# The front of a streaming-encoder kernel on one core: w_ada and x loads alternated, one shift sum moved to VectorE, two powers joined

## Chip, core and metric

The kernel runs on one core of a Trainium2 chip. The metric is the device time of one execution in microseconds. Before the change three runs took 1591.05, 1592.59 and 1591.18 us, with a median of 1591.18. The engines carry these names in the profile: PE is TensorE (matrix products; PEld is its loading of weights), DVE is VectorE, ACT is ScalarE, POOL is GpSimd, SP is SyncE, which here only issues DMAs.

## The reference

One inference step of a two-branch streaming encoder layer, over 1024 prompt rows and 32 sample rows, with D = 1024. What the change touches is the start: the modulation by the condition vector c, and the first normalised input h of the input projection.

```python
def rmsnorm(x, g):
    xf = x.astype(jnp.float32)
    y = xf * lax.rsqrt(jnp.mean(xf * xf, axis=-1, keepdims=True) + EPS)
    return (y * g.astype(jnp.float32)).astype(x.dtype)

def trunk_layer(x, c, ...):
    mod = jax.nn.silu(c) @ w_ada + b_ada
    sh1, sc1, gt1, sh2, sc2, gt2 = jnp.split(mod[:, None, :], 6, axis=-1)

    h = rmsnorm(x, g_mix) * (1 + sc1) + sh1
    u = h @ w_in
    ...
```

Behind this stand a chunk-band attention, an mLSTM memory, their merge, an output projection and a SwiGLU block, each of which the change leaves as it is. There are two condition vectors: one for the 1024 prompt rows, one for the 32 sample rows.

## The kernel before

x is held transposed: eight "features" of 128 channels lie on the partitions (KD = 8), and the 1056 rows of both sequences lie along the free axis, cut into three tiles of 352 (TILES). The first two tiles together, 704 columns, are the early part (CUT = 704); the last 352 columns are the late part, whose last 32 belong to the sample sequence.

The front (`first_units`) does this:

- **Loads.** SP issues them in the order in which they are written. `load_ada` (L248) loads one feature of w_ada as two DMAs of 512 KB: part 0 holds the scale's weights, part 1 the shift's. `xTs[j][:, :CUT]` (L265) is the early part of feature j of x, 352 KB. `load_first` (L255) loads half of each of the first three weight blocks of w_in, and L270 the late columns of x.
- **Shift and scale.** `ada_sums(j, part, pt)` (L321) sums one part of one feature on TensorE: eight matrix products of 128x128, each in two records of the profile, with silu(c) broadcast as the moving operand (L324). `ada_done(j)` (L328) lets ScalarE evict scale (`s1`, L329) and shift (`sh1`, L330).
- **Row norms.** `square_sum` squares a feature on ScalarE (L300) and adds it on VectorE (L302). `token_sums` sums over the partitions on TensorE (L307), `token_roots` (L310) divides on VectorE (L315 to L318) and takes the power -0.5 on GpSimd (L319). The early 704 rows form two groups of three columns, the late ones a third. `spread` transposes the roots (L230) and ScalarE copies them to RB (L233).
- **Weights.** Products of f32 operands are made in three passes from a high and a low part. `first_high` (L426) writes the high part on ScalarE, `first_low` (L430) the low part on VectorE.
- **h.** `scaled_x` (L338 on VectorE; L340 on GpSimd for the sample's 32 columns) multiplies x by scale and root, `high_h` (L348; L350 and L351 for the sample) adds the shift on ScalarE and writes the high part, `low_h` (L357; L359) the low part.
- **Products.** `products(k, q)` (L480) makes pass q of feature k for the first three weight blocks and both early tiles. The features run k = 0 to 7. In the code of the loop stand, between the passes, the scaled rows of feature k + 2, the low parts of k + 1, the squares of the late columns, and from k = 3 on the late roots and the late part of h. Then come the late products and `put_k`, `put_v`, `put_q`, which evict on ScalarE and VectorE (L605, L608, L610, L646, L692, L708, L710); then units of further blocks (L405), transposes of v (L680), the head splits (L668, L671), and attention (L800 and behind).

The order on TensorE, ScalarE, VectorE and GpSimd is the order in which the code is written. Each engine works through its own list in order and waits at an instruction until what it needs is there. Tiles of the pool `slots` (16 of them, named `s` in the profile) and PSUM tiles of the pool `mm` (three) are used again when their last reader is done.

## Time and profile before

| | us |
|---|---|
| median of three runs | 1591.18 |
| the profiled execution, its own time | 1591.2 |
| its span, first to last instruction | 1589.5 |
| first matrix product | 5.14 |
| token sums of the early rows (L307) | 29.69 |
| first product with h (L480) | 35.73 |
| sums of feature 7 (L324 into psS), begin | 37.15 |
| late products begin (psS, L480) | 64.60 |

The profile is of one execution. A row of the timeline gives the start of a group of like instructions, its length, the engine, the source line, the operation, the tile written and the tiles read, and in brackets how long the engine stood idle before it and what ended that. The span is the time from the first to the last instruction; the execution's own time is 1.7 us longer, for what lies around it. The same difference is used for the forecast.

### The profile page before, as it was taken

Reading aid. Unit: us, or ns where it says so; the run is one execution under the profiler, and the core shown is the slowest. Engines: PE = TensorE matmul, PEld = TensorE weight load, DVE = VectorE, ACT = ScalarE, POOL = GpSimd, SP = SyncE. Lnnn points to the kernel's source line nnn. Section 1 sums busy time; section 2 is a strip of 40 time slices with the busy share of each in tenths; the row PEclk is TensorE's granted clock in tenths of the full one; section 3 lists DMA queues with packets and bytes.
Section 4 is the critical chain, followed back from the end, with each engine's and each line's share of the span. In section 5 each row is a group of like instructions: output and inputs, shape, how many; then the busy total and the mean of one; then the engine's idle time right before and its main releaser. Section 6 shows DMA issues by size and latency. Waiting matters only on the chain.

```text
span 1589.5 us, 27294 instructions
## 1 busy us (share of the span) xinstructions
PE 1566.5 (99%) x10197; PEld 1549.4 (97%) x10197; DVE 1104.4 (69%) x2276; ACT 788.3 (50%) x1743; POOL 422.1 (27%) x439
## 2 busy tenths in 40 slices
PE   8999999999999999999999999999999999999997
PEld 8999999999999999999999999999999999999997
DVE  3765565556766835446655699898898986799755
ACT  4765554544555545444434656544445444545443
POOL 0433343342223311000012100665565750000000
PEclk9999999999999999999999999999999999999999
DMA  9322233343132323685353312223222227427444
GB/s 373 98 78 83 88 98 101 96 131 107 41 91 74 91 74 100 122 271 172 114 156 112 94 55 67 82 69 105 69 86 89 68 86 250 137 80 250 131 136 156
DMA packets 176337, 186.03 MB, mean 117 GB/s; under 512 B 11750, under 2 KB 141450, under 8 KB 176206
## 3 DMA queue, kind: packets, MB, share of 16 engines
q1 hardware_dynamic: 173542, 182.45, 36.6%
q10 hardware_dynamic: 2664, 1.85, 0.4%
q8 instruction: 80, 1.31, 0.4%
q14 instruction: 51, 0.42, 0.1%
HBM read 150.11 MB, written 34.17 MB: 116 GB/s over the span
## 4 chain that ended last, share of the span: by engine, by line
PE 91%; DVE 3%; ACT 2%; issue 2%; DMA 2%; POOL 1%; ACTq 0%; SPq 0%; DVEq 0%; POOLq 0%
PE mm L405 41%; PE psb L1875 18%; PE mm L1875 11%; PE psb L2257 3%; PE mm L954 3%; PE mm L2257 2%; PE psV L859 2%; PE psb L2121 2%; PE psS L800 2%; PE psT L827 1%; PE mm L2121 1%; DMA s<-in_w_ada_dram 1%; DMA s<-in_x_dram 1%; PE psV L1188 1%; PE psT L1190 1%
## 5 line engine op out<-in xcount | busy, mean ns | idle before, releaser
L405 PE MATMUL mm<-s,wsp 128*128 128x352 f32 x4104 | 687.2, 324 | 0.1
L405 PEld LDWEIGHTS mm<-s,wsp 128*128 128x128 f32 x4104 | 657.3, 188 | 1.9 <-issue 0.4
L368 DVE TENSOR_TENSOR wsp<-wraw,wsp 128x512 fp32r<-128x512 f32 (+1 forms) x280 | 236.4, 861 | 117.3 <-ACT wsp L367 114.1
L1875 PE MATMUL psb<-s,wsp 128*128 128x352 f32 x1611 | 271.7, 322 | 1.5 <-DVE wsp L368 0.8
L367 ACT ACTIVATE wsp<-wraw 128x512 fp32r<-128x512 f32 x336 | 199.5, 617 | 139.9 <-PE psb L1875 43.0
L1875 PEld LDWEIGHTS psb<-s,wsp 128*128 128x128 f32 x1611 | 260.6, 188 | 2.1 <-DVE wsp L368 1.1
L1875 PE MATMUL mm<-s,wsp 128*128 128x352 f32 x933 | 159.3, 322 | 0.0
L1875 PEld LDWEIGHTS mm<-s,wsp 128*128 128x128 f32 x933 | 151.2, 188 | 0.5 <-DVE wsp L368 0.5
L820 POOL TENSOR_SCALAR st<-st,mx 128x640 f32<-128x640 f32 (+5 forms) x72 | 53.5, 743 | 183.4 <-DVE mx L819 165.4
L1281 DVE CUSTOM_DVE_ANT_0 junk<-wa,t 128x512 bf16<-128x512 f32 x128 | 94.8, 741 | 5.6 <-DMA wa<-in_w_mod_dram 4.6
L368 POOL TENSOR_TENSOR wsp<-wraw,wsp 128x512 fp32r<-128x512 f32 x56 | 74.5, 1351 | 52.5 <-ACT wsp L367 50.2
L814 DVE CUSTOM_DVE_ANT_0 st<-psS,bias 128x640 f32<-128x640 f32 (+5 forms) x72 | 44.5, 618 | 57.4 <-PE psS L800 43.5
L815 ACT ACTIVATE st<-st,mx 128x640 f32<-128x640 f32 (+5 forms) x72 | 47.9, 666 | 64.4 <-DVE mx L814 64.2
L1822 POOL TENSOR_TENSOR t<-t,sl 128x352 f32<-128x352 f32 x19 | 18.4, 967 | 212.8 <-ACT sl L1820 212.8
L834 ACT ACTIVATE pT<-psT 128x640 fp32r<-128x640 f32 (+3 forms) x80 | 38.6, 493 | 64.2 <-PE psT L827 51.7
L2230 POOL TENSOR_TENSOR fst<-fst,mhalf 128x6 f32<-128x6 f32 x1 | 2.3, 2315 | 221.1 <-DVE fst L2229 221.1
L839 DVE TENSOR_TENSOR pT<-psT,pT 128x640 fp32r<-128x640 f32 (+3 forms) x80 | 44.0, 558 | 21.4 <-ACT pT L834 21.3
L1494 POOL TENSOR_TENSOR wraw<-wraw,raw 128x512 f32<-128x512 f32 x33 | 55.8, 1705 | 0.9
L954 PE MATMUL mm<-s,s 128*128 128x264 f32 (+3 forms) x432 | 54.5, 283 | 0.0
L2257 PE MATMUL psb<-s,wsp 128*128 128x352 f32 x330 | 54.2, 324 | 0.0
L2257 PEld LDWEIGHTS psb<-s,wsp 128*128 128x128 f32 x330 | 53.1, 188 | 0.1
L954 PEld LDWEIGHTS mm<-s,s 128*128 128x128 f32 (+1 forms) x432 | 51.9, 179 | 0.5
(374 smaller groups left out, 2462.0 us busy)
## 6 DMA issues: line engine op xcount, KB each, us to landing
wraw<-in_w_in_dram SPq DMA_DIRECT2D x37, 512.0 KB, 3.6
wraw<-in_w_gate_up_dram SPq DMA_DIRECT2D x33, 512.0 KB, 3.9
wa<-in_w_mod_dram SPq DMA_DIRECT2D x64, 256.0 KB, 2.7
wraw<-in_w_down_dram SPq DMA_DIRECT2D x32, 512.0 KB, 4.5
a_d<-t SPq DMA_DIRECT2D x22, 528.0 KB, 2.7
g_d<-t SPq DMA_DIRECT2D x16, 528.0 KB, 5.1
t<-g_d SPq DMA_DIRECT2D x16, 528.0 KB, 4.6
s<-in_w_ada_dram SPq DMA_DIRECT2D x16, 512.0 KB, 7.7
```

The lines of the kernel that those rows point to most:

```text
L367: act.activation(dst[:, 0], src, AF.Copy)
L368: eng.tensor_tensor(dst[:, 1], src, f(dst[:, 0]), op=ALU.subtract)
L405: pe.matmul(pt[:, :hi - lo], wt[(w0 + k) // 4][:, a, (w0 + k) % 4], xt[k][:, b, lo:hi], start=(k == 0 and q == 0), stop=(k == n - 1 and q ...
L814: dve.tensor_tensor_reduce(so, sv, bi, -1.0, 3.0e38, ALU.add, ALU.min, mx[:n, 1:2])
L815: act.activation(st[:n, :w], st[:n, :w], AF.Exp, bias=mx[:n, 1:2], scale=-1.0, accum_out=mx[:n, 2:3])
L820: pool.tensor_scalar(st[:n, :w], st[:n, :w], mx[:n, 3:4], 1.0, op0=ALU.mult, op1=ALU.mult)
L954: pe.matmul(pt[:n, :wd], hs[k][:, a, i * P:i * P + n], whl[b][:, k, :wd], start=(k == 0 and q == 0), stop=(k == KD - 1 and q == 2))
L1281: dve.tensor_tensor_reduce(junk, wa, crow[:, c], 1.0, 0.0, ALU.mult, ALU.add, at)
L1494: self.eng.tensor_tensor(a(dst), a(x), a(y), op=op)
L1875: pe.matmul(acc, wt[:, a, k], x[k][:, b], start=(start and not onto and k == 0 and q == 0), stop=(stop and k == 3 and q == 2), skip_group_ ...
L2121: pe.matmul(acc, wt[k // 4][:, u, k % 4], piece_of[k, i][:, v], start=(k == 0 and q == 0), stop=(k == KP - 1 and q == 2))
L2257: pe.matmul(acc, wt[(k - k0) // 4][:, u, (k - k0) % 4], piece_of[k, 2][:, v], start=(k == 0 and q == 0), stop=(k == NF - 1 and q == 2))
```

## The change

Four things are edited.

1. The loads of w_ada and x alternate. `load_ada(n)` now issues one half of a feature; the table `x_behind` says behind which half a row of x is issued. Part 1 of feature 7 comes last, behind the second halves of the first weights, and ahead of it a new DMA brings silu(c) of both sequences, broadcast to all partitions (`silb`, 1 MB). The squares are spread over the features by the table `squares`.
2. The shift of feature 7 is no longer summed by TensorE. Its weights are laid out anew by the host (output channel on the partition), and `shift_sum` multiplies them by `silb` and sums along the free axis on VectorE, one pass for each sequence, at k = 3 and k = 4 of the products. `ada_done(7)` evicts the scale alone.
3. `powers` takes the power of both early groups in one operation of six columns. The late group keeps its own.
4. The three `first_high` and `first_low` of the first halves now stand ahead of `spread`, and the scaled rows and high parts of feature 0 behind the second sums of feature 6.

```diff
--- before.py
+++ after.py
@@ -245,27 +245,28 @@
     def in_block(c):
         return w_in[(c - GA) // P + 28 if c >= GA else c // P]
 
-    def load_ada():
-        j = len(was)
-        wa = slot([P, 2, D])
-        for i in range(2):
-            sp.dma_start(wa[:, i], w_ada[i, j])
-        was.append(wa)
+    def load_ada(n):
+        j, i = divmod(n, 2)
+        if i == 0:
+            was.append(slot([P, 2, D]))
+        sp.dma_start(was[j][:, i], w_ada[i, j])
+
+    def load_x(j):
+        sp.dma_start(xTs[j][:, :CUT], x_t[j][:, :CUT])
 
     def load_first(half):
         for raw, c in zip(first_ws, first_cols):
             sp.dma_start(raw[:, 4 * half:4 * half + 4], in_block(c)[:, 4 * half:4 * half + 4])
 
     sq2 = slot([P, 2, T])
-    for _ in range(5):
-        load_ada()
-    for j in range(KD):
-        if j == 5:
-            load_ada()
-        sp.dma_start(xTs[j][:, :CUT], x_t[j][:, :CUT])
-    load_ada()
+    x_behind = {1: 0, 2: 1, 4: 2, 5: 3, 7: 4, 8: 5, 9: 6, 10: 7}
+    for n in range(13):
+        load_ada(n)
+        if n in x_behind:
+            load_x(x_behind[n])
     load_first(0)
-    load_ada()
+    load_ada(13)
+    load_ada(14)
     for i, xp in enumerate(xTp):
         sp.dma_start(xp[:, :, CUT:], x_t[2 * i:2 * i + 2].rearrange("n p t -> p n t")[:, :, CUT:])
     load_first(1)
@@ -276,6 +277,7 @@
     silu1 = cp.tile([P, 2], F32, name="silu1")
     sh1 = cp.tile([P, 2, KD], F32, name="sh1")
     s1 = cp.tile([P, 2, KD], F32, name="s1")
+    shs = cp.tile([P, 2], F32, name="shs")
     gm1 = cols[:, R_GMIX:R_GMIX + KD]
     psA, psH, psS = ps_t(), ps_v(), ps_s()
     tok = psS[:, 512:]
@@ -316,7 +318,10 @@
         else:
             dve.tensor_scalar(x[:, 0, :2], p3[:, :2], 1.0 / D, EPS, op0=ALU.mult, op1=ALU.add)
             dve.tensor_scalar(x[:m, 0, 2:], p3[:m, 2:], 1.0 / D, EPS, op0=ALU.mult, op1=ALU.add)
-        pool.tensor_tensor(x[:, 1], x[:, 0], mhalf[:, :3], op=ALU.pow)
+
+    def powers(t0, t1):
+        x = roots[:, :, 3 * t0:3 * t1]
+        pool.tensor_tensor(x[:, 1], x[:, 0], mhalf[:, :3 * (t1 - t0)], op=ALU.pow)
 
     def ada_sums(j, part, pt):
 
@@ -325,8 +330,16 @@
                       was[j][:, part, k * P:(k + 1) * P], csil[:, k].unsqueeze(1).to_broadcast([P, DH, 2]),
                       start=(k == 0), stop=(k == KD - 1), skip_group_check=True)
 
+    def shift_sum(j, c, silb):
+
+        at = shs[:, c:c + 1]
+        dve.tensor_tensor_reduce(was[j][:, 0], was[j][:, 1], silb[:, c], 1.0, 0.0, ALU.mult, ALU.add, at)
+        dve.tensor_tensor(sh1[:, c, j:j + 1], at, cols[:, R_ADA + j:R_ADA + j + 1], op=ALU.add)
+
     def ada_done(j, pt):
         act.activation(s1[:, :, j], pt[:, :2], AF.Identity, scale=gm1[:, j:j + 1], bias=gb1[:, j:j + 1])
+        if j == KD - 1:
+            return
         act.activation(sh1[:, :, j], pt[:, P:P + 2], AF.Identity, bias=cols[:, R_ADA + j:R_ADA + j + 1])
 
     hs = []
@@ -436,21 +449,22 @@
         silu_cols()
         act.activation(crows, crows, AF.Silu)
         act.dma_start(sil_d, crows)
+        silb = slot([P, 2, D])
+        sp.dma_start(silb, bass.AP(sil_d.tensor, sil_d.offset, [[0, P], [D, 2], [1, D]]))
+        load_ada(15)
+        squares = ((0,), (1,), (2, 3), (4,), (5, 6), (7,))
         for j in range(6):
             pt = mmt()
             ada_sums(j, 0, pt)
             ada_sums(j, 1, pt)
-            if j < 3:
-                ada_done(j, pt)
-            else:
-                n = {3: 2, 4: 6, 5: KD}[j]
-                for i in range({3: 0, 4: 2, 5: 6}[j], n):
-                    square_sum(i, 0, CUT)
-                ada_done(j, pt)
+            for i in squares[j]:
+                square_sum(i, 0, CUT)
+            ada_done(j, pt)
         token_sums(0, CUT, 0, DH)
         groups = [(0, 3 * P), (3 * P, CUT)]
         for i, (lo, hi) in enumerate(groups):
             token_roots(i, hi - lo, 3 * DH * i, DH)
+        powers(0, 2)
         pt = mmt()
 
         def spread(i):
@@ -458,19 +472,17 @@
             bcast_cols(RB, roots[:, 1, 3 * i:3 * i + 3], [min(P, hi - a) for a in range(lo, hi, P)], lo)
 
         ada_sums(6, 0, pt)
-        first_high(0, 0)
-        first_high(1, 0)
+        for i in range(3):
+            first_high(i, 0)
+        for i in range(3):
+            first_low(i, 0)
         spread(0)
         spread(1)
-        scaled_x(0, *early[0])
-        scaled_x(0, *early[1])
-        first_high(2, 0)
-        high_h(0, *early[0])
-        high_h(0, *early[1])
         ada_sums(6, 1, pt)
+        for t in range(2):
+            scaled_x(0, *early[t])
+            high_h(0, *early[t])
         ada_done(6, pt)
-        for i in range(3):
-            first_low(i, 0)
         pts = [[mmt(), mmt()], [psA[:, :512], psA[:, 512:]], [mmt(), psH]]
         last = [psS[:, :512], tok]
 
@@ -498,7 +510,6 @@
             for i in range(3):
                 product(0, i, 0, t)
         ada_sums(7, 0, psS)
-        ada_sums(7, 1, psS)
         scaled_x(1, 0, CUT)
         low_h(0, 0, CUT)
         high_h(1, 0, CUT)
@@ -539,10 +550,13 @@
             if k == 3:
                 token_sums(late[0], NT, NT, 32)
                 token_roots(2, NT, NT, 32)
+                powers(2, 3)
                 W.loaded = W.split_n = 3
                 W.load(6)
                 early_loads.append(cache_loads())
                 early_loads.extend(rel_bias_tile(h) for h in range(2))
+            if k in (3, 4):
+                shift_sum(7, k - 3, silb)
             if k == 4:
                 for i, n in enumerate((P, P, NT - 2 * P)):
                     pe.transpose(tok[:, i * P:i * P + n], roots[:n, 1, 6 + i:7 + i].to_broadcast([n, P]), ident[:n, :n])
@@ -2309,7 +2323,9 @@
             a = a.T.reshape(KD, P, T)
         elif name == "w_ada":
             a = _np.asarray(inputs["w_ada"])[0, :, :2 * D].reshape(KD, P, 2, KD, P)
-            a = a.transpose(2, 3, 1, 0, 4)[::-1].reshape(2, KD, P, D)
+            last = a[:, :, 0, -1].reshape(D, P).T
+            a = a.transpose(2, 3, 1, 0, 4)[::-1].reshape(2, KD, P, D).copy()
+            a[1, -1] = last
         else:
             a = _np.asarray(inputs[name])
         if name == "rel_bias":
```

The list of SP at the start, before. The tiles s_106, s_109, s_112, s_115, s_118, s_126 and s_132 are features 0 to 6 of w_ada, s_98 to s_101 hold two features of x each; "x2" is two DMAs.

```order
L252 DMA s_112<-in_w_ada_dram 128x1024 x2
L252 DMA s_115<-in_w_ada_dram 128x1024 x2
L252 DMA s_118<-in_w_ada_dram 128x1024 x2
L265 DMA s_98<-in_x_dram 128x704 x2
L265 DMA s_99<-in_x_dram 128x704 x2
L265 DMA s_100<-in_x_dram 128x704
L252 DMA s_126<-in_w_ada_dram 128x1024 x2
L265 DMA s_100<-in_x_dram 128x704
L265 DMA s_101<-in_x_dram 128x704 x2
L252 DMA s_132<-in_w_ada_dram 128x1024 x2
```

The same list now, from feature 3 on (s_119, s_123, s_128 and s_132 are features 3 to 6 of w_ada).

```order
L252 DMA s_119<-in_w_ada_dram 128x1024 x2
L255 DMA s_100<-in_x_dram 128x704
L252 DMA s_123<-in_w_ada_dram 128x1024
L255 DMA s_100<-in_x_dram 128x704
L252 DMA s_123<-in_w_ada_dram 128x1024
L255 DMA s_101<-in_x_dram 128x704
L252 DMA s_128<-in_w_ada_dram 128x1024
L255 DMA s_101<-in_x_dram 128x704
L252 DMA s_128<-in_w_ada_dram 128x1024
L252 DMA s_132<-in_w_ada_dram 128x1024
```

The last row of x stood behind all of feature 5 and now stands ahead of feature 5's second half, which became the last load of the first six features and of x.

VectorE around the early roots, before: roots, then the scaled rows of feature 0 (s_98, which wait for RB), then the three low parts of the weights (wsp, wsp and s_350), then feature 1.

```order
L315 TENSOR_SCALAR roots<-psS_155 128x3
L317 TENSOR_SCALAR roots<-psS_155 128x2
L318 TENSOR_SCALAR roots<-psS_155 64x1
L338 SCALAR_TENSOR_TENSOR s_98<-s_98,s_152,t_148 128x352 x2
L430 TENSOR_TENSOR wsp_332<-wraw_102,wsp_332 128x512
L430 TENSOR_TENSOR wsp_335<-wraw_103,wsp_335 128x512
L430 TENSOR_TENSOR s_350<-wraw_104,s_350 128x512
```

And now.

```order
L317 TENSOR_SCALAR roots<-psS_155 128x3
L319 TENSOR_SCALAR roots<-psS_155 128x2
L320 TENSOR_SCALAR roots<-psS_155 64x1
L443 TENSOR_TENSOR wsp_334<-wraw_102,wsp_334 128x512
L443 TENSOR_TENSOR wsp_337<-wraw_103,wsp_337 128x512
L443 TENSOR_TENSOR s_340<-wraw_104,s_340 128x512
L351 SCALAR_TENSOR_TENSOR s_98<-s_98,s_151,t_147 128x352 x2
```

The low parts have moved in between the roots and the scaled rows, to the time in which GpSimd raises the roots to their power.

VectorE at k = 3 to 5 of the products, before: the low part of feature 4 (s_456), the late roots, and the scaled rows and low parts of the next features.

```order
L357 SCALAR_TENSOR_TENSOR s_456<-s_100,sh_151,s_456 128x704
L317 TENSOR_SCALAR roots<-psS_155 128x2
L318 TENSOR_SCALAR roots<-psS_155 96x1
L338 SCALAR_TENSOR_TENSOR s_101<-s_101,s_152,t_148 128x704
L357 SCALAR_TENSOR_TENSOR s_488<-s_100,sh_151,s_488 128x704
L338 SCALAR_TENSOR_TENSOR s_101<-s_101,s_152,t_148 128x704
```

The same place now; `ISA` is the pass of `shift_sum` (s_138 is feature 7 of w_ada, s_183 is `silb`) and the reading of its accumulator.

```order
L370 SCALAR_TENSOR_TENSOR s_449<-s_100,sh_150,s_449 128x704
L319 TENSOR_SCALAR roots<-psS_155 128x2
L320 TENSOR_SCALAR roots<-psS_155 96x1
L336 ISA s_138,shs<-s_138,s_183 128x1024
L336 ISA shs 128x1
L337 TENSOR_TENSOR sh_150<-shs,cols 128x1
L351 SCALAR_TENSOR_TENSOR s_101<-s_101,s_151,t_147 128x704
L370 SCALAR_TENSOR_TENSOR s_481<-s_100,sh_150,s_481 128x704
L336 ISA s_138,shs<-s_138,s_183 128x1024
L336 ISA shs 128x1
L337 TENSOR_TENSOR sh_150<-shs,cols 128x1
L351 SCALAR_TENSOR_TENSOR s_101<-s_101,s_151,t_147 128x704
```

Six instructions have come in, in two groups; nothing else has changed its place there. On TensorE, the sums of feature 7 behind the first six products have gone from 16 products to 8.

## The prediction

> **What bounds the kernel now.** The page comes first: busy time, share of the span and instructions of each engine.
>
> ```profile
> PE 1566.5 (99%) x10197; PEld 1549.4 (97%) x10197; DVE 1104.4 (69%) x2276; ACT 788.3 (50%) x1743; POOL 422.1 (27%) x439
> ```
>
> TensorE bounds nearly everything, so a change in the first 60 us is worth what it does to TensorE's position, until another engine's chain crosses TensorE's. Hence the second view, busy time by stretch (columns: PE, PEld, DVE, ACT, POOL, each with its count; then clock, DMA share, GB/s). The stretches are the feature sums of the shifts and scales, the row norms up to the first product, VectorE's run through the products, ScalarE's run behind it, and the start of attention.
>
> ```profile
> 5.14:28.50 23.36, 23.36 (x192) 23.17 (x192) 5.31 (x6) 9.15 (x19) 0.00 (x0) 1.00 1.03 407
> 28.50:35.70 7.20, 6.01 (x49) 5.62 (x50) 2.81 (x8) 3.87 (x9) 1.70 (x2) 1.00 1.04 387
> 45.07:59.44 14.37, 13.95 (x90) 13.66 (x90) 14.12 (x23) 6.36 (x10) 5.40 (x2) 1.00 0.33 111
> 59.59:76.20 16.61, 16.61 (x108) 16.57 (x107) 11.42 (x21) 16.09 (x43) 11.79 (x23) 1.00 0.14 49
> 76.57:92.69 16.12, 14.29 (x89) 13.65 (x88) 10.57 (x24) 9.80 (x21) 5.83 (x9) 1.00 0.29 83
> ```
>
> The reader is to see three limits in a row. Up to 28.5 us TensorE is full and the DMA engines are full as well (share 1.03 at 407 GB/s). From 45.07 to 59.44 VectorE is full (14.12 of 14.37). From 59.59 to 76.20 ScalarE is full (16.09 of 16.61). TensorE loses 1.2 us between 28.5 and 35.7 and 1.8 us after 76.57. The chain of waits shows where the first loss is.
>
> ```profile
> 16.65 9.03 DMA s<-in_x_dram
> 25.76 0.79 ACT s L300
> ...
> 28.65 0.90 DVE t L302
> ...
> 29.69 1.57 PE psS L307 x12
> 31.36 0.17 DVE roots L315
> 31.61 1.70 POOL roots L319 x2
> ```
>
> The last rows of x land late, are squared and added, and the token sums start at 29.69, though the sums of feature 5 were done at 28.5. The list of waits gives that wait, and three later ones that tie TensorE to the other engines.
>
> ```profile
> PE psS L307 <- DVE t L302: 1.2, 1, 1.2
> ACT s L350 <- POOL s L340: 2.3, 1, 2.3
> PEld mm L405 <- DVE s L671: 0.4, 1, 0.4
> PE psT L827 <- DVE pT L839: 1.8, 1, 1.8
> ```
>
> The second row is the hinge of this forecast. The timeline shows it (start, duration, engine, line, operation; in brackets the idle time before it).
>
> ```profile
> 55.53 4.44 POOL L340 TENSOR_TENSOR s<-s,t 128x32 f32<-128x32 f32 x3 [1.15 <-ACT t L549]
> 60.55 0.26 POOL L340 TENSOR_TENSOR s<-s,t 128x32 f32<-128x32 f32 x1
> 58.90 0.54 DVE L338 SCALAR_TENSOR_TENSOR s<-s,s,t 128x320 f32<-128x320 f32 x1
> 59.59 0.41 ACT L350 ACTIVATE s<-s,sh,s 128x32 f32<-128x32 f32 x1 [2.27 <-POOL s L340]
> 77.08 1.73 PE L405 MATMUL mm<-s,wsp 128*128 128x352 f32 x9
> ```
>
> Three operations of 0.26 us took 4.44 us on GpSimd: the first got through only when VectorE paused, at 58.90 + 0.54 = 59.44. ScalarE stood still for it, started its run at 59.59, and was still behind when TensorE, at 77.08, waited for an eviction. So from 45 to 77 us the end is set by VectorE's run, then by ScalarE's, and TensorE has nothing to spare there.
>
> **The change, step by step.** First the loads. TensorE's own pace for a feature is seen in ScalarE's evictions, and the last load of x in the answer for its tile.
>
> ```profile
> 14.24 0.35 ACT L329 ACTIVATE s<-mm,gb,cols 128x2 f32<-128x2 f32 x1 [3.06 <-PE mm L324]
> 17.82 0.35 ACT L329 ACTIVATE s<-mm,gb,cols 128x2 f32<-128x2 f32 x1 [3.07 <-PE mm L324]
> ```
>
> ```profile
> L265 SPq DMA_DIRECT2D s<-in_x_dram x1: 328/328/328, 18.5 to 18.5; - x1
> DMA to landing us min/median/max: 9.0/9.0/9.0
> ```
>
> A feature takes 17.82 - 14.24 = 3.58 us, half a feature 1.79. The last x lands at 18.5 + 9.0 = 27.5, and by then the same bytes have been loaded in either order (six features of w_ada, eight rows of x), because the stretch is full of DMA. In the new order the last of them is the second half of feature 5. TensorE then starts that half at about 27.55 and the token sums at 27.55 + 1.79 = 29.34: **0.35 us** earlier, not the 1.2 us of the wait. The wait for x turns into waits for weights, some 0.4 us ahead of each of the last two halves. Bounds: 1.2 us earlier if the weights come in time after all, 0 if the alternation costs as much as it saves. The squares cost nothing: ScalarE is busy 9.15 of 23.36 us here. The x row ahead of the last half leaves room for its square and addition (0.79 + 0.90) beside TensorE's 1.79.
>
> Second, the powers and the splits. Both powers become one operation on six columns, and the three splits of the first weights (L430) now stand directly behind the roots on VectorE, where GpSimd's power runs.
>
> ```profile
> 31.51 0.14 DVE L318 TENSOR_SCALAR roots<-psS 64x1 f32<-64x1 f32 x1
> 35.12 1.28 DVE L430 TENSOR_TENSOR wsp<-wraw,wsp 128x512 fp32r<-128x512 f32 x2
> 36.32 0.68 DVE L430 TENSOR_TENSOR s<-wraw,s 128x512 fp32r<-128x512 f32 x1
> 1541.22 1.28 DVE L368 TENSOR_TENSOR wsp<-wraw,wsp 128x512 fp32r<-128x512 f32 x2
> 1541.38 2.31 POOL L2230 TENSOR_TENSOR fst<-fst,mhalf 128x6 f32<-128x6 f32 x1 [221.07 <-DVE fst L2229]
> 52.73 0.94 DVE L338 SCALAR_TENSOR_TENSOR s<-s,s,t 128x704 f32<-128x704 f32 x1
> 52.89 1.49 POOL L319 TENSOR_TENSOR roots<-roots,mhalf 128x3 f32<-128x3 f32 x1 [19.58 <-DVE roots L318]
> ```
>
> ```profile
> L1652 POOL TENSOR_TENSOR rs<-rs,mhalf x3: 1012/1019/1220, 834.3 to 899.2; 128x4 f32<-128x4 f32 x3
> ```
>
> Three columns took 0.85 us each time at 31.61, four take 1.02, so six undisturbed would be about 0.85 + 3 x 0.16 = 1.3 us, less than the two operations' 1.70. But the one six-column power of this trace started 0.16 us behind two such splits and took 2.31: it ended 1.19 us after the second. At 52.89 the power of three took 1.49, ending 0.71 after VectorE's first operation, although another followed at once. In the new order ScalarE writes the high parts while TensorE makes the token sums, so all three splits are ready or nearly so when VectorE's roots end, at 31.51 + 0.14 - 0.35 = 31.30. I take 2.31, the row with the same operation, the same neighbours and the same predecessor. The ends are 1.3 (nothing blocks) and 1.88 (the three splits, 35.12 to 37.00) + 1.19 - 0.15 = 2.9.
>
> The Trainium skill, "SBUF — State Buffer", section "Who interferes with whom", says that a VectorE instruction with two SBUF inputs contends with a GpSimd instruction that reads SBUF, and that the one that issues second blocks until the first finishes. By that rule the power waits for one split, not for two or three; the row at 52.89 agrees with it, those at 55.53 and 1541.38 show longer blocks.
>
> Before, the transposes behind the powers started 33.07 - 31.65 = 1.42 us after the roots (row below), held by TensorE's own sums of feature 6. Now they start 0.1 + 2.31 + 0.05 = 2.46 after them: +1.04. With the -0.35, the transposes are **0.69 us later**. What was behind the splits is now ahead: VectorE reaches the scaling of feature 1 earlier, but TensorE does not need it earlier.
>
> ```profile
> 33.07 0.93 PE L230 MATMUL mm<-ident,roots 128*128 128x128 f32 x6
> 37.15 3.73 PE L324 MATMUL psS<-csil,s 128*128 128x128 f32 x32
> ```
>
> Third, feature 7's shift leaves TensorE: 16 of 32 records of 3.73 us, **-1.86 us**, at a place where TensorE had nothing to wait for. TensorE stands at 0.69 - 1.86 = -1.17 us when the products go on, and every engine's work that waits for the scale of feature 7 moves along.
>
> Fourth, that shift is summed by VectorE in two passes over 128x1024, inside the run that fills 45.07 to 59.44. Nearest rows, kept apart by form:
>
> ```profile
> L1281 DVE CUSTOM_DVE_ANT_0 junk<-wa,t 128x512 bf16<-128x512 f32 x128 | 94.8, 741 | 5.6 <-DMA wa<-in_w_mod_dram 4.6
> L1281 DVE DVE_READ_ACCUMULATOR2_ANT sums<- 128x1 f32 x128 | 10.3, 80 | 0.0
> L1110 DVE SCALAR_TENSOR_TENSOR s<-t,cols,s 128x1024 f32<-128x1024 f32 x24 | 32.9, 1371 | 3.4 <-ACT s L1103 3.3
> ```
>
> The same operation over 512 takes 0.74, another form over 1024 takes 1.37. With the accumulator read (0.08) and the bias behind it, a pass is one of 1024's and hardly less than 1.2: I take 1.35 for all of it, 2 x 1.35 = **+2.7 us**; bounds 2.4 and 3.0. ScalarE loses the eviction of that shift.
>
> ```profile
> 41.18 0.26 ACT L330 ACTIVATE sh<-psS,cols 128x2 f32<-128x2 f32 x1
> 45.07 0.69 DVE L430 TENSOR_TENSOR wsp<-wraw,wsp 128x512 fp32r<-128x512 f32 x1 [1.05 <-ACT wsp L426]
> ```
>
> VectorE's run starts at 45.07 behind ScalarE, so it starts some 0.2 us earlier. Nothing in the run can absorb the other 2.5: it has 14.37 - 14.12 = 0.25 us of gaps. Queued behind the two passes on VectorE are the scaled rows and low parts of features 5 to 7 and of the late third. TensorE waits for none of those today; that it still doesn't with 2.5 us less is assumed. But GpSimd's L340 waits until VectorE pauses, ScalarE's run waits for L340, and TensorE at 77.08 for ScalarE. So the place that holds TensorE moves by -1.17 + 2.5 = **+1.3 us**, while TensorE alone would have been 1.2 early. After 77 us the chain alternates between ScalarE, GpSimd and VectorE up to TensorE's 1.8 us wait at L827, and carries the shift on; later TensorE is full.
>
> The DMAs: the two rows of silu cost 1 MB more on SP's queue, about 2.6 us at some 400 GB/s, ahead of the bias, cache and w_mod loads. These serve the blocks behind the products, and after 45.07 the DMA engines are a third busy: nothing.
>
> The sum is made on the profiled execution: span 1589.5, its own time 1591.2, which is the median of the three runs. 1591.2 + 1.3 = **1592.5 us**; with the power's ends +0.3 to +1.9, 1591.5 to 1593.1. A measurement of this kernel tells about 0.2%, 3.2 us, from no change, so the forecast is no measurable change.
>
> **The rivals.** One split only: the power goes through at the first boundary, as at 52.89. Then it ends one split, 0.6 us, earlier, the place at 77.08 moves by +0.7: 1591.9. For it speaks that row, against it the other two. By the rule of the Trainium skill named above, this is what happens.
>
> VectorE's new passes let GpSimd in: behind each of them stands an accumulator read and an addition that waits for it, a pause the run did not have. Then L340 is done before ScalarE needs it, ScalarE's run loses its wait of 2.27 us at 59.59 and is 2.5 - 2.27 = 0.2 late instead of 2.5, and the place at 77.08 moves by -1.17 + 0.2 = -0.9: 1590.3. Against it: only the second pause falls where L340 stands ready, one L340 fits into it, and the next one meets a full VectorE again.
>
> On the slow side: the power is blocked by all three splits, since none of them waits for anything. It decides from the moment the third high part is written before the second split ends. Price 0.6 more than forecast: +1.9, 1593.1.
>
> The change doesn't do what it says: the weights land in time and the whole 1.2 us is won ahead of the token sums, 0.85 more than summed: +0.5, 1591.7. Against it the DMA share of 1.03. The clock that TensorE was granted is 1.00 in every stretch above, so a slower clock is no rival.
>
> **How the numbers follow.** Forecast 0.37, one split 0.21, GpSimd let in 0.18, three splits 0.12, weights in time 0.04, something else 0.08 (0.03 of it faster, 0.05 slower). The first five lie between 1590.3 and 1593.1; with the runs' own spread of 1591.05 to 1592.59, about 0.7 each way, the range is 1589.6 to 1593.8. Faster than 1588.0 lies beyond all gains without any price (-1.2 - 1.86 = -3.1): 0.03. Slower than 1594.4 needs a stall that is not in the sum, such as TensorE running dry among the products: 0.05. The same: 0.92.
>
> **What would show it.** In the profile of the changed kernel: token sums near 29.3 with short waits of TensorE for w_ada ahead of them; a power of six columns of about 2.3 us beside the splits; 16 records less on TensorE's sums of feature 7; two VectorE passes of about 1.2 us between 50 and 56; L340 released only when VectorE pauses, near 60.8; TensorE's wait for an eviction near 77 grown from the 0.4 us of the list to about 2.7. It is wrong if TensorE does not wait there, if the power takes 1.3, or if token sums start by 28.6.

## The result, and the profile after

| | before | changed |
|---|---|---|
| median of 22 runs each, us | 1591.18 (1590.87 to 1593.10) | 1588.91 (1588.71 to 1589.61) |
| span of the profiled execution, us | 1589.5 | 1587.2 |

The ratio is 0.9985, with a 95% interval of 0.9978 to 0.9991: faster by 0.15%. That is less than the 0.2% that the prediction took as the least it could tell from no change, but the interval does not reach 1. The time lies 3.6 us below the forecast of 1592.5 and 0.7 below the range's lower end of 1589.6.

The page's first line, busy time of each engine, answers to that of before: TensorE has 16 records (eight products) less, VectorE 3.2 us of work more.

```profile
PE 1564.9 (99%) x10181; PEld 1547.8 (98%) x10181; DVE 1107.6 (70%) x2282; ACT 788.5 (50%) x1742; POOL 420.5 (26%) x438
```

Busy time by stretch, the same five places as before (columns: PE, PEld, DVE, ACT, POOL; then clock, DMA share, GB/s).

```profile
5.53:28.50 22.97, 22.97 (x185) 22.81 (x186) 6.25 (x7) 9.23 (x19) 0.00 (x0) 1.00 1.03 406
28.50:35.78 7.28, 7.01 (x61) 6.45 (x59) 3.69 (x9) 3.88 (x9) 1.65 (x1) 1.00 1.05 384
43.19:58.02 14.83, 14.28 (x93) 13.99 (x91) 14.52 (x26) 6.18 (x10) 3.61 (x4) 1.00 0.54 171
58.02:74.60 16.58, 16.58 (x107) 16.54 (x107) 13.16 (x25) 16.06 (x44) 11.36 (x21) 1.00 0.16 49
74.97:91.09 16.12, 14.28 (x89) 13.64 (x88) 10.57 (x24) 9.79 (x21) 5.83 (x9) 1.00 0.28 83
```

The same three limits follow each other, but VectorE's run now begins at 43.19 instead of 45.07 and ScalarE's at 58.02 instead of 59.59, and from 74.97 on the kernel is the one of before, 1.6 us earlier. TensorE's timeline in the changed kernel shows where that was won (start, duration, operation, wait before it); the last two rows, behind the dots, are the kernel before at the same places as the rows of 52.83 and 91.09.

```profile
29.35 1.48 PE L309 MATMUL psS<-ones,t 128*128 128x64 f32 x12
33.08 0.96 PE L230 MATMUL mm<-ident,roots 128*128 128x128 f32 x6 [0.27 <-POOL roots L324]
37.20 1.94 PE L329 MATMUL psS<-csil,s 128*128 128x128 f32 x16
52.83 0.52 PE L562 MATMUL psS<-ident,roots 128*128 128x128 f32 x3 [0.55 <-POOL roots L324]
75.49 1.42 PEld L418 LDWEIGHTS mm<-s,wsp 128*128 128x128 f32 x9 [0.37 <-DVE s L685]
91.09 0.41 PE L841 MATMUL psT<-ident,st 128*128 128x128 f32 x2 [1.76 <-DVE pT L853]
...
54.43 0.52 PE L548 MATMUL psS<-ident,roots 128*128 128x128 f32 x3 [0.42 <-POOL roots L319]
92.69 0.41 PE L827 MATMUL psT<-ident,st 128*128 128x128 f32 x2 [1.77 <-DVE pT L839]
```

The token sums start at 29.35 instead of 29.69, but the transposes behind the norms at 33.08, against 33.07 before: the power beside the splits, shown with the errors of the prediction, gave the 0.34 back. The sums of feature 7 take 1.94 instead of 3.73 us. From there TensorE is 1.6 to 1.7 us ahead: late transposes 52.83 against 54.43, the wait for an eviction 75.49 against 77.08, attention's transposes 91.09 against 92.69. (These are attention's second transposes, which end TensorE's wait of 1.8 us; a single one stands ahead of them, at 86.78 now and 88.38 before. Some of the expectations below call the second ones the first.) The wait at 75.49 has not grown; it was forecast to grow to 2.7 us. Behind 91 us another 0.7 us is gained that no wait names; the last paragraph of the experiments takes that up.

Why the wait did not grow is seen on VectorE, GpSimd and ScalarE, timeline again.

```profile
53.90 1.22 DVE L336 CUSTOM_DVE_ANT_0 s<-s,s 128x1024 f32<-128x1024 f32 x1
55.04 0.08 DVE L336 DVE_READ_ACCUMULATOR2_ANT shs<- 128x1 f32 x1
55.16 0.16 DVE L337 TENSOR_TENSOR sh<-shs,cols 128x1 f32<-128x1 f32 x1
55.23 0.95 DVE L351 SCALAR_TENSOR_TENSOR s<-s,s,t 128x704 f32<-128x704 f32 x1
...
54.46 1.83 POOL L353 TENSOR_TENSOR s<-s,t 128x32 f32<-128x32 f32 x3 [1.69 <-ACT t L563]
...
57.55 0.57 ACT L361 ACTIVATE s<-s,sh 128x320 fp32r<-128x320 f32 x1 [0.45 <-DVE s L351]
58.02 0.40 ACT L363 ACTIVATE s<-s,sh,s 128x32 f32<-128x32 f32 x1
```

An independent operation on VectorE starts before the one ahead has ended (55.23 against 55.16 + 0.16 = 55.32). The addition that needs the accumulator starts 0.04 us behind it (55.16 against 55.04 + 0.08). That is the pause. (A boundary, below, is the passage from one VectorE operation to the next.) GpSimd's three scaled sample columns (L353, L340 before), which took 4.44 us in the kernel before, took 1.83 here, and ScalarE goes from 57.55 into its run without the wait of 2.27.

### The profile page after: what moved, and what is told of

It is laid out like the page before. It is cut to its first block, busy times and chain, and to the rows that moved or that the text cites. A ratio compares the mean times of both kernels' runs of the same rounds, so it can differ in the third digit from the quotient of the medians.

```text
span 1587.2 us, 27275 instructions
## 1 busy us (share of the span) xinstructions
PE 1564.9 (99%) x10181; PEld 1547.8 (98%) x10181; DVE 1107.6 (70%) x2282; ACT 788.5 (50%) x1742; POOL 420.5 (26%) x438
## 4 chain that ended last, share of the span: by engine, by line
PE 92%; DVE 3%; ACT 2%; issue 2%; POOL 1%; DMA 0%; ACTq 0%; POOLq 0%; DVEq 0%
PE mm L418 41%; PE psb L1889 18%; PE mm L1889 11%; PE psb L2271 3%; PE mm L968 3%; PE mm L2271 2%; PE psV L873 2%; PE psb L2135 2%; PE psS L814 2%; PE mm L329 2%; PE psT L841 1%; PE mm L2135 1%; PE psV L1202 1%; PE psT L1204 1%; PE psT L1199 1%
```

## The experiments

Eighteen kernels ran, in five groups, each group on one chip beside the kernel before. The intervals of the ratios are about 0.0009 wide to each side, 1.4 us, so differences of some tenths are read from the traces: the last column is the time from the first transposes behind the norms to attention's transposes (92.69 in the kernel before, 91.09 in the changed one), which leaves out how the loads happened to go (the transposes behind the norms start at 32.67 to 33.62). Each such time is that of one execution. no_passes and the kernels with nopause in their names leave out the sum of feature 7's shift, so they are probes and not versions to use. In nopause_tiny1 the last column holds a stretch of slower clock, shown at the end.

| kernel | median, us | before on that chip | ratio, 95% interval | transposes to attention, us |
|---|---|---|---|---|
| before | 1591.18 | | | 59.62 |
| changed | 1588.91 | 1591.18 | 0.9985 (0.9978, 0.9991) | 58.01 |
| no_passes | 1588.87 | 1591.08 | 0.9987 (0.9978, 0.9996) | 57.85 |
| passes_early | 1589.26 | 1591.08 | 0.9988 (0.9979, 0.9997) | 58.05 |
| b_pause | 1590.93 | 1591.08 | 0.9998 (0.9989, 1.0007) | 59.62 |
| two_powers | 1589.87 | 1591.08 | 0.9992 (0.9983, 1.0001) | 59.25 |
| passes_nopause | 1591.16 | 1591.11 | 1.0002 (0.9993, 1.0011) | 60.00 |
| passes_late | 1588.91 | 1591.11 | 0.9987 (0.9978, 0.9996) | 57.85 |
| no_shift | 1591.22 | 1591.11 | 1.0000 (0.9992, 1.0009) | 59.73 |
| splits_behind | 1590.05 | 1591.11 | 0.9993 (0.9984, 1.0002) | 59.28 |
| loads_old | 1590.38 | 1591.61 | 0.9989 (0.9980, 0.9998) | 58.02 |
| power_apart | 1589.75 | 1591.61 | 0.9986 (0.9977, 0.9994) | 58.83 |
| third_pass | 1590.36 | 1591.61 | 0.9989 (0.9980, 0.9998) | 59.05 |
| pass_tail | 1589.61 | 1591.61 | 0.9984 (0.9975, 0.9992) | 57.77 |
| nopause_768 | 1591.16 | 1591.60 | 0.9996 (0.9987, 1.0006) | 59.74 |
| nopause_896 | 1591.33 | 1591.60 | 0.9998 (0.9989, 1.0007) | 59.86 |
| nopause_tiny1 | 1592.25 | 1591.60 | 1.0003 (0.9993, 1.0012) | 61.15 |
| nopause_tiny3 | 1592.05 | 1591.60 | 1.0001 (0.9992, 1.0011) | 60.19 |
| nopause_dep4 | 1590.12 | 1591.35 | 0.9993 (0.9984, 1.0003) | 58.14 |
| early_nopause | 1590.43 | 1591.35 | 0.9992 (0.9982, 1.0001) | 58.15 |

**Is it the pauses that let GpSimd in, and what is it worth?** Theory A, spelled out in the first expectation, says yes; theory C says that GpSimd was only unlucky in the kernel before. The edits are to the changed kernel, but for the last, which is to the kernel before.

```diff
 no_passes:
-            if k in (3, 4):
-                shift_sum(7, k - 3, silb)
+            if k == 3:
+                dve.tensor_copy(sh1[:, :, 7], cols[:, R_ADA + 7:R_ADA + 8].to_broadcast([P, 2]))
 passes_nopause: as no_passes, and
+            if k in (3, 4):
+                dve.scalar_tensor_tensor(was[7][:, 0], was[7][:, 1], shs[:, 0:1], silb[:, k - 3], op0=ALU.mult, op1=ALU.add)
 passes_early:
-            if k in (3, 4):
-                shift_sum(7, k - 3, silb)
+            if k == 3:
+                for c in range(2):
+                    shift_sum(7, c, silb)
 b_pause:
+            if k == 5:
+                dve.tensor_tensor(shp[:, 0:1], cols[:, 0:1], cols[:, 1:2], op=ALU.add)
+                dve.tensor_tensor(shp[:, 1:2], shp[:, 0:1], cols[:, 1:2], op=ALU.add)
```

no_passes:

> The changed kernel without its two VectorE passes (the shift of feature 7 is then its bias alone; that part of the computation is left out). Theory A, GpSimd is let in where VectorE has a short pause, and the accumulator read with the addition behind it is one: with the passes the pause goes too, so the sample columns' scaling on GpSimd is starved again, one operation of 3 to 4 us as in the kernel before, until VectorE's run ends near 59.44 - 1.88 = 57.6; ScalarE waits for it some 1 to 2 us and starts its run near 57.7, against 58.02 with the passes: 2.6 us less work on VectorE bring at most 0.3 us, about 1588.7. Theory C, GpSimd gets through at the first or second boundary between any two VectorE operations and the 4.03 us of the kernel before was bad luck: no operation there over 1 us, ScalarE's run starts 2.6 earlier at about 55.4, and TensorE gains its 0.24 us of waiting at 75.5 and perhaps some of its 1.76 us at 91.1: 1587 to 1588.7.

passes_nopause:

> The changed kernel with its two VectorE passes replaced by plain multiply-adds over the same 128x1024 at the same places, with no accumulator read and no dependent addition (the shift of feature 7 is its bias alone; that sum is left out). VectorE's run keeps its length, only the pauses go. Theory A: GpSimd's first scaled sample columns starve again from about 54.4 until VectorE's run ends near 59.44 - 1.88 + 2.6 = 60.2; ScalarE starts its run at 60.3 and not at 58.02, and since ScalarE had only 0.33 us of spare time at 74.97, TensorE waits some 1.7 to 2.0 us longer near 75.5: 1590.6 to 1590.9. Rival: with VectorE's operations falling otherwise GpSimd gets through at a boundary, as it did with the passes put earlier: 1588.9 to 1589.2.

passes_early:

> The changed kernel with both passes at the third feature (VectorE about 51 to 53.4), so that their pauses lie before the late columns' scale reaches GpSimd at 54.4. VectorE has the same work in the same run. Theory A: the first scaled sample columns on GpSimd take 3 to 5 us again, until VectorE pauses near 59 to 60, ScalarE's run starts at 59.5 to 60.5 instead of 58.02 and TensorE's wait near 75.5 grows from 0.24 to about 1.7 to 2.5: 1590.4 to 1591.2. Theory C: three operations under 1 us each, ScalarE as before at 58.0, 1588.9. The forecast on record (VectorE's run length alone decides) gives no difference between the two orders either: 1588.9.

b_pause:

> The kernel before with two tiny additions on 128x1, the second dependent on the first, put on VectorE behind the low part of feature 6 (about 56.2), where GpSimd's first scaled sample columns wait. Theory A: they get in at about 56.3 and not at 59.44; ScalarE's wait of 2.27 at 59.59 goes and its run starts near 57.4. TensorE gains its wait of 0.2 to 0.4 us near 77 at once; how much of its 1.76 us at 92.7 goes with it is open: 1589.4 to 1591.0, most likely near 1590.9. Theory C: nothing moves, 1591.2 to 1591.4.

Timelines of no_passes (two rows) and passes_nopause (three):

```profile
53.70 4.42 POOL L353 TENSOR_TENSOR s<-s,t 128x32 f32<-128x32 f32 x3 [1.15 <-ACT t L563]
57.73 0.41 ACT L363 ACTIVATE s<-s,sh,s 128x32 f32<-128x32 f32 x1 [2.26 <-POOL s L353]
...
54.40 6.15 POOL L354 TENSOR_TENSOR s<-s,t 128x32 f32<-128x32 f32 x3 [1.49 <-ACT t L566]
60.17 0.42 ACT L364 ACTIVATE s<-s,sh,s 128x32 f32<-128x32 f32 x1 [2.26 <-POOL s L354]
76.39 0.55 PE L697 MATMUL mm<-ident,t 128*128 128x128 f32 x3 [1.64 <-ACT t L663]
```

Take the passes away, and the starving comes back (4.42 us): 2.6 us less work on VectorE buy 0.16 us up to attention and nothing that can be measured in the time. Keep VectorE's work and take only the pauses away, and GpSimd takes 6.15 us, ScalarE starts 2.1 later and TensorE waits 1.64 us for it: the time is 2.25 us above that of the changed kernel and equal to before; up to attention it is 1.99 us, and 0.38 more than before. This is the stall that the prediction had forecast; it exists, and the pauses avoid it. b_pause, two rows:

```profile
55.49 1.29 POOL L341 TENSOR_TENSOR s<-s,t 128x32 f32<-128x32 f32 x3 [1.15 <-ACT t L550]
72.29 0.93 ACT L609 ACTIVATE s<-psS 64x352 fp32r<-64x352 f32 x2 [1.21 <-PE psS L481]
```

The pair of tiny additions ends the starving in the kernel before as well (1.29 instead of 4.44), but TensorE gains nothing (59.62 both): ScalarE now waits 1.21 us for TensorE at 72.29. In the kernel before, the starving was only just covered. passes_early, the addition that ends the last pause and GpSimd's three:

```profile
53.47 0.16 DVE L337 TENSOR_TENSOR sh<-shs,cols 128x1 f32<-128x1 f32 x1
55.84 1.81 POOL L353 TENSOR_TENSOR s<-s,t 128x32 f32<-128x32 f32 x3 [3.03 <-ACT t L564]
```

Theory A had forecast starving here, at 1590.4 to 1591.2. GpSimd's three took 1.81 us, although the last pause was over at 53.5, and the time is 1589.26; so the narrow form of theory A, that only a pause during GpSimd's wait counts, fell, and the last group takes that up.

**What each other part is worth.** Edits to the changed kernel; "as before" is the code of the diff's minus lines.

```diff
 splits_behind: first_high, first_low, spread, scaled_x and high_h as before, powers(0, 2) kept
 two_powers: the same, and powers(i, i + 1) behind each token_roots
 power_apart: powers(i, i + 1) behind each token_roots, first_low ahead as in the change
 no_shift: ada_sums(7, 1, psS) back, no shift_sum, no silb
 loads_old: ten halves of w_ada, then x with two halves in it, squares as before
```

two_powers:

> The changed kernel with the power and the splits as before (two operations of three columns right behind their roots, the splits of the first weights behind the scaling): the loads and the shift alone are left of the change. The powers should take 0.87 and 0.86 us, so the transposes should start at 33.08 - 0.35 = 32.7, since the joined power of 1.65 behind the roots ate what the loads had won. TensorE's position from there on 0.35 earlier: 1588.55. Rival: ScalarE's or VectorE's runs do not follow, since the splits now stand behind the scaling again: 1588.9, and the 0.35 shows as a longer wait of TensorE near 75.5.

splits_behind:

> The changed kernel with the joined power, and the splits of the first weights behind the scaling as before. The power of six columns has no VectorE operation beside it and should take about 1.3 us instead of 1.65: transposes near 32.7, 0.35 earlier. But the splits fill VectorE between 34.7 and 36.6 again: its run starts about 0.8 later, as it did with two powers (44.00 against 43.19), TensorE waits some 1.1 us for the late power near 53, and the end is as with two powers: 1589.8. Rival: only the two powers cost there, and the end is at 1588.6.

Timeline of splits_behind, GpSimd, VectorE and TensorE:

```profile
31.27 1.34 POOL L324 TENSOR_TENSOR roots<-roots,mhalf 128x6 f32<-128x6 f32 x1 [29.75 <-DVE roots L320]
...
44.06 0.69 DVE L443 TENSOR_TENSOR wsp<-wraw,wsp 128x512 fp32r<-128x512 f32 x1 [0.53 <-DMA wa<-in_w_mod_dram]
...
48.78 0.80 PE L309 MATMUL psS<-ones,t 128*128 128x32 f32 x6 [0.43 <-DVE t L297]
53.69 0.52 PE L564 MATMUL psS<-ident,roots 128*128 128x128 f32 x3 [1.12 <-POOL roots L324]
```

Undisturbed, the power takes 1.34 us and the transposes start at 32.67, 0.4 earlier. But VectorE's run starts at 44.06 instead of 43.19, and TensorE, early by the shift it no longer sums, now waits 0.43 us for VectorE's late squares and 1.12 for the late power. Both kernels lose 1.2 us from the transposes to attention, and 0.4 of it was won ahead of them. splits_behind came out as forecast and its rival is out. For two_powers the forecast of 1588.55 failed (1589.87): its rival named the cause, VectorE's run, but the wait shows at 53 us (1.11 for the late power) and not near 75.5. So the splits ahead of the scaling, priced at nothing, carry half of the gain: they fill VectorE's wait for the norms, and only then can its run start as early as TensorE needs.

power_apart:

> The changed kernel with the two powers as two operations again, each behind its roots, and the splits still ahead of the scaling, so beside both. Each power of three columns is blocked until a split ends: the first to about 32.5, the second to about 33.6; transposes near 33.6 and not 33.08, VectorE's and TensorE's work behind them 0.5 later: 1589.4. Rival: the lock is had once and kept, both end near 33.1 as the joined one: 1588.9.

```profile
34.12 0.63 PE L230 MATMUL mm<-ident,roots 128*128 128x128 f32 x3 [0.65 <-POOL roots L324]
```

Measured: the two powers took 1.37 and 1.22 us beside the splits, the second three transposes started at 34.12, and 0.8 us more passed up to attention. In the time it is 0.4 against the changed kernel, each beside its own before, which lies inside the intervals. By the trace the joined power is worth 0.8 us once the splits stand there.

no_shift:

> The changed kernel with feature 7's shift summed by TensorE again and no passes on VectorE: the loads, the joined power and the splits ahead of the scaling are left. Transposes at 33.08, as in both kernels, and the products go on at 40.65; from there TensorE has what VectorE's earlier run gives. If the shift's 1.73 us is the whole gain: 1591.2 less at most 0.2, 1591.0. Rival: the splits ahead of the scaling are worth something by themselves, because VectorE's run starts earlier and the late row sums and their power (TensorE waits 0.42 for it in the kernel before) with it: 1590.5 to 1590.8.

Measured 1591.22 against 1591.11, and 59.73 against 59.62 us up to attention: the first forecast held. Without the shift's move, loads, power and splits together give nothing that can be measured; VectorE then waits 1.8 us for ScalarE at 42.1, and its run starts at 44.94. The parts do not add up one by one: the shift's move without the splits gives 1.06 to 1.21 us, the splits without the shift nothing, both 2.27.

loads_old:

> The changed kernel with the loads in the order of before (and the squares spread over the features as before). The last rows of x land last again: token sums near 29.7, roots near 31.35, and everything behind them, the power of 1.65 and VectorE's run too, 0.35 later than in the changed kernel: 1589.25. Rival: the loads' 0.35 is lost anyway in the wait for the power or for the late power: 1588.9.

The token sums started at 29.66 (changed: 29.35, before: 29.69), and everything up to attention 0.40 later than in the changed kernel, as expected; the time was 1.23 below its own before, where 1.9 was expected. The other 0.6 lies behind attention's transposes, where its trace took 1.0 us longer than that of the changed kernel. The gain of the loads is not steady: with the alternating loads the token sums started at 29.12 to 29.88 in seventeen traces (half of them by 29.36), with the old order at 29.66 to 29.69 in three.

**VectorE's length, and a better place for the passes.**

```diff
 third_pass: behind shift_sum
+            if k == 4:
+                dve.tensor_tensor_reduce(was[6][:, 0], was[6][:, 1], silb[:, 0], 1.0, 0.0, ALU.mult, ALU.add, shx)
 passes_late:
+            if k in (4, 5):
+                shift_sum(7, k - 4, silb)
 pass_tail: shift_sum(7, 0, silb) at k == 4, and
+        shift_sum(7, 1, silb)
         for k in range(7, KD + 2):
             late_h(k)
```

third_pass:

> The changed kernel with a third pass over 128x1024, of feature 6, behind the second; nothing reads its sum. GpSimd is let in at the second pass's pause as before, so only VectorE's length counts: ScalarE starts its run 1.25 later, near 59.3, of which its spare 0.33 us at 74.97 takes a part; TensorE near 75.5 is 0.9 later: 1589.8. If TensorE had more to spare than that there: 1588.9; if the whole length counts: 1590.2.

passes_late:

> The changed kernel with the first pass one feature later and the second right ahead of the late columns' scaling, so that no pass stands behind the late roots on VectorE. The late power should take 1.49 as in the kernel before and not 1.77, and TensorE's wait of 0.55 at 52.8 should be about 0.27 less; the second pass's pause lies near 55.5 to 56, where GpSimd's scaled sample columns wait, so ScalarE starts its run near 58 as before: 1588.6. Rival: ScalarE's high part of feature 7, which now waits for the first pass, is later and TensorE near 75.5 with it: 1588.9 to 1589.5.

pass_tail:

> The changed kernel with the first pass one feature later, as in the run with both passes later, and the second behind the loop over the features, where VectorE is idle a third of the time. Late power 1.5 and TensorE's wait at 52.6 down from 0.55 to 0.28; the pause of the first pass near 53.5 lets GpSimd in; ScalarE's run starts some 1.3 earlier than with both passes in VectorE's run, so the wait of 0.27 near 75.3 that took the gain back there does not come: 1588.6. Rival: TensorE's wait for attention's first transposes near 91 takes it: 1588.9.

Timelines of TensorE, third_pass (first row) and passes_late (the other two):

```profile
75.94 0.55 PE L697 MATMUL mm<-ident,t 128*128 128x128 f32 x3 [0.76 <-ACT t L663]
...
52.32 0.52 PE L562 MATMUL psS<-ident,roots 128*128 128x128 f32 x3 [0.28 <-POOL roots L324]
75.27 1.72 PE L418 MATMUL mm<-s,wsp 128*128 128x352 f32 x9 [0.27 <-DVE s L685]
```

A third pass costs 1.04 us up to attention and 1.0 in the time, against 0.9 forecast: of the 1.22 us by which it lengthens VectorE's run, 1.04 reach TensorE, with GpSimd let in. Put later, the passes free the late power (the wait falls from 0.55 to 0.28), but 0.16 of it is all that is left at attention; pass_tail has 0.24 there. Neither is measurably faster than the changed kernel.

**What lets GpSimd in.** All edits are to passes_nopause (early_nopause: both multiply-adds at k == 3).

```diff
 nopause_768, nopause_896: the second multiply-add over 768 or 896 elements
 nopause_tiny1, nopause_tiny3: ahead of it, with m = 1 or 3
+                for i in range(m):
+                    dve.tensor_tensor(shx[:, i:i + 1], cols[:, i:i + 1], cols[:, 8:9], op=ALU.add)
 nopause_dep4: ahead of it
+                dve.tensor_tensor(shx[:, 0:1], cols[:, 0:1], cols[:, 8:9], op=ALU.add)
+                dve.tensor_tensor(shx[:, 1:2], shx[:, 0:1], cols[:, 8:9], op=ALU.add)
```

nopause_768:

> The kernel without pauses, with the second plain multiply-add over 768 of 1024 elements (the shift of feature 7 is its bias alone, as there), so that VectorE's next boundary comes 0.40 us after GpSimd's first scaled sample columns start and not 0.71. Theory P, the phase decides: ages of 0.36 to 0.49 were let in at the first boundary in other kernels, so no operation takes over 1 us, ScalarE starts near 57.7 and the time is 1588.7 to 1589.0. Theory A, only a pause lets GpSimd in beside a full VectorE: one operation of 5.4 us, ScalarE near 59.9, 1590.9.

nopause_896:

> As before with 896 elements: the first boundary 0.55 us after GpSimd's operation starts, an age that no run has shown yet. Theory P: let in, if what counts is to be under 0.7: 1588.9. Theory A: 5.6 us, 1591.0.

nopause_tiny1:

> The kernel without pauses, with one addition on 128x1 ahead of the second multiply-add, over before GpSimd's operation starts; the boundary moves from 0.71 to about 0.78 us after its start. Theory P: 0.78 and 0.79 were let in in other kernels, so here too: ScalarE near 58.1, 1589.0. Theory A: starved for 5.8 us, 1591.2.

nopause_tiny3:

> The same with three such additions: the boundary about 0.92 us after the start, not seen yet. Theory P has no number for it: either 1589.1 or 1591.3. Theory A: starved, 1591.3.

nopause_dep4:

> The kernel without pauses, with two additions on 128x1 ahead of the second multiply-add, the second dependent on the first: a pause that is over some 0.4 us before GpSimd's scaled sample columns start. Theory Q, a pause a little earlier is enough for GpSimd to get the next ordinary boundary: let in at about 55.1, ScalarE's run near 58.2, 1.8 to 2.0 us faster than with one or three independent additions, so 0.3 above to 2.0 below the kernel before on the same chip, about 1.7 below. Theory A in its narrow form, only a pause that falls while GpSimd waits counts: starved for 5.8 us, 0.1 to 0.6 above the kernel before.

early_nopause:

> The kernel with both passes put earlier, with plain multiply-adds in their place and so without pauses (the shift of feature 7 is its bias alone). Theory Q: it was the pauses at 52.1 and 53.4 that made GpSimd's operation at 55.84 pass at an ordinary boundary; without them it starves until VectorE's run ends near 60, ScalarE's run starts at 60.2, and the time is that of the kernel before, within 0.3. Rival: at that place it is let in without any pause, because it comes later in the run: 1.8 below the kernel before, as with the passes there.

Timelines of nopause_tiny3 (two rows), nopause_dep4 (four) and early_nopause (two):

```profile
53.81 0.29 DVE L564 TENSOR_TENSOR shx<-cols 128x1 f32<-128x1 f32 x3
54.37 6.36 POOL L355 TENSOR_TENSOR s<-s,t 128x32 f32<-128x32 f32 x3 [1.49 <-ACT t L570]
...
54.19 0.15 DVE L563 TENSOR_TENSOR shx<-cols 128x1 f32<-128x1 f32 x1
54.37 0.16 DVE L564 TENSOR_TENSOR shx<-shx,cols 128x1 f32<-128x1 f32 x1
54.45 1.28 DVE L566 SCALAR_TENSOR_TENSOR s<-s,shs,s 128x1024 f32<-128x1024 f32 x1
54.74 2.81 POOL L355 TENSOR_TENSOR s<-s,t 128x32 f32<-128x32 f32 x3 [1.49 <-ACT t L570]
...
51.41 2.59 DVE L562 SCALAR_TENSOR_TENSOR s<-s,shs,s 128x1024 f32<-128x1024 f32 x2
56.21 1.81 POOL L354 TENSOR_TENSOR s<-s,t 128x32 f32<-128x32 f32 x3 [2.81 <-ACT t L566]
```

The four that only shift VectorE's boundaries (nopause_768, nopause_896, nopause_tiny1 and nopause_tiny3) all starve, for 5.5 to 5.9 us in the first operation: the moment of the boundary does not decide, and theory P falls. Three independent additions (a run of 0.29 us without a gap) don't help; two of which the second depends on the first (0.03 us between 54.34 and 54.37) do, although the pause is over 0.3 us before GpSimd's operation starts. It then passes at the next ordinary boundary, as theory Q said. Up to attention it is 58.14 us instead of the 60.19 of nopause_tiny3, which differs from it in the dependence and one addition more; the median is 1.2 below its before instead of 0.45 above. early_nopause was meant to be without a pause and was not: its two multiply-adds write the same rows, and took 2.59 us instead of the 2.47 of two overlapping ones, so there is a gap between them at 52.7. Over all twenty traces: in the eight without a dependent pair of operations on VectorE between the start of the late power and the end of its full run, GpSimd's scaled sample columns starved; in the twelve with one they got in at that pause or at the next ordinary boundary behind it, even where it was over 3 us back (52.7 and 56.21 in early_nopause). That a pause so far back still counts is seen, but how is open, and so early_nopause did not give the test that it was made for.

**What stays open in the sum.** From attention's transposes to the start of TensorE's last matmul the time is 1487.5 us before and 1487.1 in the changed kernel, and 1487.1 to 1488.1 in the other traces, but for pass_tail with a slower clock there (1488.7). Behind that matmul come 9.3 us before and 9.0 in the changed kernel, and 8.9 to 9.3 in the others. So the 0.7 us gained behind 91 may be the scatter of the two profiled executions; but the medians of 22 runs keep 2.27 us, and what makes up the rest is not known.

## Why the prediction was wrong

- **What bounds the kernel.** The three limits in a row hold. One reading was half right: that ScalarE "was still behind when TensorE, at 77.08, waited for an eviction". The eviction of 75.65 (L668) did stand in ScalarE's run without idle time, and TensorE waited 0.36 us for what followed it on VectorE (L671). But the next eviction already waited for TensorE. The row of the kernel before, and one of b_pause, where ScalarE's run starts 1.6 us earlier:

```profile
76.57 0.60 ACT L668 ACTIVATE s<-mm 128x512 fp32r<-128x512 f32 x1 [0.34 <-PE mm L680]
...
78.55 0.09 PEld L631 LDWEIGHTS mm<-ident,t 128*32 128x32 f32 x1 [0.39 <-ACT stg L639]
```

ScalarE had made up its 2.27 us with 0.34 to spare. In b_pause the wait near 77 is gone, but TensorE waits 0.39 us for ScalarE at 78.55 instead, and nothing is left of the gain at attention.

- **Loads, -0.35:** measured -0.34 at the token sums (29.69 to 29.35). Right in the trace; that it came within 0.01 is luck, since the start moves by 0.8 us over the seventeen traces.
- **Power, +0.69 at the transposes:** measured +0.01. The term was mis-sized. The splits and the power in the changed kernel:

```profile
31.15 1.28 DVE L443 TENSOR_TENSOR wsp<-wraw,wsp 128x512 fp32r<-128x512 f32 x2
31.38 1.65 POOL L324 TENSOR_TENSOR roots<-roots,mhalf 128x6 f32<-128x6 f32 x1 [29.86 <-DVE roots L320]
```

Beside the three splits it took 1.65 us, not 2.31. It was held for 0.31 over its undisturbed 1.34, which is about the time to the end of the first split; the rival with one split had that. The row at 52.89 was the right neighbour and not the one at 1541.38. That one is no accident, since it shows 2.31 in all twenty traces; why it is held past the first split there is open. The rule of the Trainium skill, "SBUF — State Buffer", section "Who interferes with whom", is that the operation that issues second waits for the first. It gives the power of the changed kernel, but neither the row at 1541.38 nor GpSimd's starving.

- **Splits, nothing:** wrong. Put back, they cost 1.2 us up to attention. The step looked at TensorE's next need only, not at where VectorE's run would start once TensorE came 1.7 us earlier.
- **Feature 7's shift off TensorE, -1.86:** measured -1.73 where the products go on (40.64 to 38.91).
- **The passes, +2.7 on VectorE:** measured 2 x 1.33 (50.84 to 52.17, 53.90 to 55.23). Right. VectorE's run began 1.88 us earlier (45.07 to 43.19) where the sum had it 1.4 earlier, with TensorE's -1.17 and 0.2 for the eviction.
- **The step that failed** is the end of the fourth: "GpSimd's L340 waits until VectorE pauses", with no pause until VectorE's run ends, hence +1.3 at 77. The passes bring the pauses themselves, and TensorE was 1.59 us early there instead. The rival said so, with a chance of 0.18 and this objection: only the second pause falls where L340 stands ready, one L340 fits into it, and the next meets a full VectorE again. Measured, all three went through in 1.83 us, since behind a pause the ordinary boundaries let GpSimd in too. With the power's 0.01 in place of 0.69 that rival gives -0.9 - 0.68 = -1.6 at 77, which is what was measured (-1.59). So of the 3.6 us between forecast and time 0.7 is the power, 2.2 this step, and 0.7 lies behind 91 us and is not explained. Without the pauses (passes_nopause) the forecast's own chain comes about, but smaller: 0.4 us later than before at attention and not 1.3, since the power's 0.68 is not lost and ScalarE's spare 0.34 is used up first.
- **DMAs, nothing:** not tried alone.

## What to carry to other kernels

Work moved off the bounding engine is worth what the next engine can follow: look where that engine idles ahead of its full run and put work there first. When GpSimd shares a stretch with a full VectorE, count VectorE's dependent pairs of operations, since a pause of 0.04 us decided about 2 us here. And before an engine is called late, look for the rows in which it waits itself.
